# Branch units of a hybrid encoder block: weight sums on VectorE, three blocks of the first branch kept in SBUF, the second branch's blocks stored from GpSimd

## The chip, the core and the metric

The kernel runs on one core of one Trainium2 chip. The metric is the device time of one execution in microseconds. A run of a kernel gives such a time; where several were made their median is quoted. The profile is of one execution, and its times count from the start of that execution's span.

## What is computed

One encoder layer on x of shape (1, 1024, 1024), float32. A single input projection gives u and v of a chunked gating branch, value a and gate g of a convolution branch, and two output gates ga and gb. Each branch ends in a multiplication with a 1024x1024 matrix:

```python
n = rms_norm(h, norm1_g[l])
z = n @ w_in[l]
z_u, z_v, z_a, z_g, z_ga, z_gb = jnp.split(z, split_at, axis=-1)
y_a = spatial_gating(jax.nn.gelu(z_u), jax.nn.gelu(z_v), sg_ln_g[l], sg_ln_b[l],
                     sg_w[l], sg_b[l]) @ w_a_out[l]
y_b = conformer_conv(z_a, z_g, cv_dw_w[l], cv_dw_b[l], cv_ln_g[l], cv_ln_b[l]) @ w_b_out[l]
merged = jax.nn.sigmoid(z_ga) * y_a + jax.nn.sigmoid(z_gb) * y_b
h = h + merged @ w_o[l]
...
h = h + (a feed-forward part with a depthwise convolution of width 3), then a last rms_norm
```

`conformer_conv` is a gated product, a depthwise convolution of width 31, a layer norm over the channels and a silu.

## The kernel before

**Number format.** Every matmul operand is kept as two parts, hi and lo, in a rounded 32-bit type: ScalarE casts the value to hi (L130), VectorE subtracts hi from the value to get lo. A product of two operands is three matmuls, hi x hi, hi x lo and lo x hi. All TensorE and VectorE instructions are recorded through one helper, so their line in the profile is L69; groups are told apart by their tiles. `a`, `w` and `s` are tiles of three pools (`abig`: 16 of 8 KB per partition, `wp`: 3 of 8 KB, `sm`: 15 of 4 KB), `bank` is PSUM. A tile `s` of 128x1024 is 512 KB.

**Projections.** A loop over `order` projects a, g, v, gates, u0 to u7 and then the last six gates, gb2 to gb7. Each projection is 48 matmuls of 128x512. A gate leaves PSUM by a sigmoid on ScalarE (L882) and goes to DRAM (L883); u goes through `evac_u`, and after each odd one `sums_out` is called.

**Branch products.** y_a and y_b are made in eight units, four of `w_a_out` on the first branch (s) and four of `w_b_out` on the second (c, the convolution). A unit covers two column tiles of the weight and is one level of Strassen-Winograd: seven products of 12 matmuls (`strassen`), 84 matmuls in all, instead of eight. Product seven of a unit is put off to stand behind the first product of the next unit. The activation operands are seven blocks, four of them sums of quarters. `sums_out` (L490) makes the sums for two of the eight row tiles with four VectorE instructions of 128x512, and stores all seven blocks to DRAM (`fb_d`) with one transfer of 256 KB and three of 512 KB (L499, L501). It is called four times for each branch: for s with GpSimd's queue, for c with SyncE's. `Blocks` loads them back (L519, two loads of 512 KB per block) and splits them to hi and lo. The block order is 0, 1, 5, 2, 3, 4, 6.

The seven weight operands of a unit are built by `Unit.load` in four steps (L555, L558, L561, L564): SyncE loads quarters of the weight, three times 512 KB and once 256 KB, and after each a GpSimd transfer of 256 KB adds another quarter or an earlier sum to one half of the tile (L566). The same class serves the units of w_o and of the feed-forward part later on.

**The convolution's layer norm** runs in the background of the projections (`conv_norm`, pieces in `bg` and `soon`): a mean by matmul, eight deviations (`dev`), the variance by matmul (`var`), the broadcast of its inverse root by matmul with `ident` (`var2`), eight normalisations `fin` with a multiplication on VectorE and a silu on ScalarE (L743), and after each pair `c_sums` with `sums_out`. A piece is put in where a running model of VectorE's clock has room (`fill`), and the matmuls of `soon` ride in a projection after its third or seventh group. So work added to VectorE earlier moves these pieces later. `conv_d` is the DRAM copy of the deviations, loaded again for `fin` (L697).

**The entry into the units.** In the last three projections `prepare(0..2)` loads s blocks and the first weights and splits them. The stores of c blocks stand in a queue `stores`, emptied after a projection and, one for each, in the `slot` that `strassen` calls after a product. In the products L610 and L617 copy a bank's half, L622 and L627 leave a negated copy in `s`; the next product into that bank waits for them.

## Time and profile before

| | before |
|---|---|
| time, median of 3 runs | 1521.07 us (1520.88 to 1525.44) |
| the profiled execution's own time | 1521.1 us |
| its span in the profile | 1519.0 us |
| TensorE busy | 1464.2 us, 96% of the span, 6633 matmuls |
| VectorE busy | 1007.9 us, 66% |
| ScalarE busy | 629.1 us, 41% |
| GpSimd busy | 165.3 us, 11% |
| SyncE's queue (q1) | 224.63 MB, 42.7% of 16 engines' span |
| GpSimd's queue (q0) | 61.88 MB, 21.8% |

TensorE is busy nearly all the time; the share is an average over stages. The page's row of slices shows full slices up to the entry of the units at about 560 us, and there lower digits for TensorE and for the granted clock, with DMA at nine tenths. The time of a group of transfers is the mean over 16 DMA engines.

### The profile page before, as it was taken

To read this page: it belongs to the slowest core of one execution; us is meant where nothing else is said; L and a number is where in the kernel's file an instruction comes from. 1 tells how busy PE (TensorE), PEld (TensorE's weight loads), DVE (VectorE), ACT (ScalarE), POOL (GpSimd) and SP (SyncE) were. 2 spreads that over 40 slices of the span, in tenths; PEclk is the share of its full clock that TensorE was granted. 3 is DMA by queue.
4 is the path that set the end of the run, shared out by engine and by line. 5 is a ranking of instruction groups with operands and counts; after the bars stand their busy time and mean duration, and the time that the engine had idled before them with its cause. 6 is when DMAs were issued, how large, how long until landed. Compare 5 with 4: busy or idle time off the path is not lost.

```text
span 1519.0 us, 17358 instructions
## 1 busy us (share of the span) xinstructions
PE 1464.2 (96%) x6633; PEld 1213.4 (80%) x6633; DVE 1007.9 (66%) x1047; ACT 629.1 (41%) x763; POOL 165.3 (11%) x200
## 2 busy tenths in 40 slices
PE   9999999999999975999999999999999999999998
PEld 7888888888888864877788888888888887878887
DVE  6899989888998563464553885555555448465545
ACT  6433233443412463353322454444444447353353
POOL 0000000000010001212100011111111211112000
PEclk9999999999999997999999999999999999999999
DMA  5343566445546889999835279777777779999743
GB/s 199 98 109 97 157 178 166 125 125 152 154 128 231 308 282 364 247 357 310 249 100 184 77 182 243 199 202 201 199 202 197 196 190 294 283 361 300 250 173 111
DMA packets 122243, 310.69 MB, mean 205 GB/s; under 512 B 11568, under 2 KB 13872, under 8 KB 122160
## 3 DMA queue, kind: packets, MB, share of 16 engines
q1 hardware_dynamic: 86112, 224.63, 42.7%
q0 software_dynamic: 27392, 61.88, 21.8%
q10 hardware_dynamic: 8656, 23.08, 3.9%
q8 instruction: 52, 0.85, 0.2%
q14 instruction: 31, 0.25, 0.1%
HBM read 199.43 MB, written 76.55 MB: 182 GB/s over the span
## 4 chain that ended last, share of the span: by engine, by line
PE 79%; DMA 7%; DVE 7%; issue 4%; ACT 3%; SPq 1%; POOL 0%; ACTq 0%; DVEq 0%; POOLq 0%
PE bank L69 79%; DVE s L69 5%; DMA s<-fb_d 2%; DMA s<-in_w_a 1%; DMA s<-in_w_b 1%; DMA fb_d<-s 1%; DVE a L69 1%; ACT a L130 1%; DMA s<-h_d 1%; DVE w L69 0%; DMA s<-in_xT 0%; DMA s<-conv_d 0%; ACT w L130 0%; ACT s L743 0%; DMA s<-in_w_down 0%
## 5 line engine op out<-in xcount | busy, mean ns | idle before, releaser
L69 PE MATMUL bank<-a,w 128*128 128x512 f32 (+1 forms) x4158 | 961.7, 391 | 43.5 <-ACT s L622 10.5
L69 PEld LDWEIGHTS bank<-a,w 128*128 128x128 f32 x4158 | 779.2, 190 | 212.2 <-ACT s L622 12.7
L69 PE MATMUL bank<-a,a 128*128 128x512 f32 (+2 forms) x1922 | 413.2, 372 | 2.7 <-ACT s L627 2.0
L69 PEld LDWEIGHTS bank<-a,a 128*128 128x128 f32 x1922 | 340.2, 188 | 68.0 <-ACT s L627 3.3
L69 DVE TENSOR_TENSOR w<-s,w 128x1024 fp32r<-128x1024 f32 (+3 forms) x144 | 162.8, 1132 | 249.7 <-ACT w L130 244.8
L69 DVE TENSOR_TENSOR a<-s,a 128x1024 fp32r<-128x1024 f32 (+2 forms) x180 | 197.7, 1123 | 144.6 <-ACT a L130 144.4
L69 DVE SCALAR_TENSOR_TENSOR s<-hb,vt,s 128x1024 f32<-128x1024 f32 x204 | 247.9, 1277 | 0.0
L130 ACT CAST w<-s 128x1024 fp32r<-128x1024 f32 (+2 forms) x143 | 139.4, 977 | 169.7 <-PE bank L69 87.8
L130 ACT CAST a<-s 128x1024 fp32r<-128x1024 f32 (+2 forms) x148 | 144.3, 995 | 74.5 <-DVE s L69 20.6
L69 DVE TENSOR_TENSOR s<-s,bank 128x1024 f32<-128x1024 f32 (+2 forms) x128 | 110.6, 882 | 36.5 <-PE bank L69 26.3
L566 POOL DMA_DIRECT2D s<-s x72 | 63.5, 881 | 363.5 <-DMA s<-in_w_up 96.0
L69 DVE TENSOR_TENSOR s<-s,s 128x1024 f32<-128x1024 f32 (+1 forms) x74 | 79.0, 1076 | 13.9 <-DMA s<-conv_d 5.1
L69 PE MATMUL bank<-w,a 128*128 128x512 f32 x384 | 87.2, 389 | 0.0
L69 PEld LDWEIGHTS bank<-w,a 128*128 128x128 f32 x384 | 72.1, 188 | 15.0
L566 POOL DMA_DIRECT2D s<-in_w_up x40 | 40.9, 1022 | 260.6 <-DMA s<-in_w_up 232.8
L446 POOL DMA_DIRECT2D s<-s x28 | 24.2, 865 | 370.6 <-ACT s L445 308.8
L69 DVE TENSOR_TENSOR csum<-csum,s 128x1024 f32<-128x1024 f32 (+2 forms) x55 | 45.7, 832 | 22.7 <-ACT s L1387 11.2
L627 ACT ACTIVATE s<-bank 128x512 f32<-128x512 f32 x36 | 21.5, 597 | 79.1 <-PE bank L69 79.1
L610 ACT COPY bank<-bank 128x512 f32<-128x512 f32 x36 | 20.6, 572 | 62.0 <-PE bank L69 61.6
L622 ACT ACTIVATE s<-bank 128x512 f32<-128x512 f32 x36 | 21.4, 594 | 58.2 <-PE bank L69 57.8
L882 ACT ACTIVATE s<-bank 128x1024 f32<-128x1024 f32 x16 | 16.4, 1025 | 69.7 <-PE bank L69 62.0
L1175 ACT ACTIVATE s<-s 128x1024 f32<-128x1024 f32 x22 | 23.3, 1061 | 38.8 <-DVE s L69 38.8
(85 smaller groups left out, 559.6 us busy)
## 6 DMA issues: line engine op xcount, KB each, us to landing
s<-in_w_up SPq DMA_DIRECT2D x64, 512.0 KB, 6.9
s<-fb_d SPq DMA_DIRECT2D x56, 512.0 KB, 9.3
s<-in_w_in SPq DMA_DIRECT2D x39, 512.0 KB, 4.4
fb_d<-s SPq DMA_DIRECT2D x36, 512.0 KB, 3.1
s<-s POOLq DMA_DIRECT2D x72, 256.0 KB, 5.7
s<-s POOLq DMA_DIRECT2D x28, 512.0 KB, 6.5
s<-in_w_down SPq DMA_DIRECT2D x24, 512.0 KB, 8.3
s<-h_d SPq DMA_DIRECT2D x24, 512.0 KB, 8.1
```

The lines of the kernel that those rows point to most:

```text
L69: return fn(*args, **kwargs)
L130: A.copy(dst_hi, src)
L446: G.dma_start(box[k % 2], p, accum_op=ALU.add)
L566: G.dma_start(r[:, 0 if i == 3 else 1], add, accum_op=ALU.add)
L610: A.copy(x[:, 1], x[:, 0])
L622: A.activation(u[:, 0], x[:, 1], AF.Copy, scale=-1.0)
L627: A.activation(u[:, 1], x[:, 1], AF.Copy, scale=-1.0)
L882: A.activation(t, ps.rearrange("p a b -> p (a b)"), AF.Sigmoid)
L1175: A.activation(t, t, AF.Gelu_apprx_tanh)
```

## The change

The change has four parts. **(1)** The eight branch units become `SumUnit`: two plain loads of 512 KB from SyncE per unit (four quarters), and the four sums by VectorE, 128x512 each, two after the split of the first pair of quarters and two after the third split. **(2)** For the s branch, `sums_out` gets `direct`: blocks 0, 1 and 5 in the numbering of the store, the first three of `ORDER`, are split where they are made (three ScalarE copies and three VectorE subtractions of 128x512 per call, four calls), into tiles that stay in SBUF; only the other four blocks are stored, with three transfers per call instead of four, and loaded. **(3)** `c_sums` stores from GpSimd's queue, and what is left in `stores` is issued before the loads behind the last projection. **(4)** `prepare` loads the fourth block and the first unit's two weight tiles, and splits them.

```diff
--- before.py
+++ after.py
@@ -487,13 +487,28 @@
     fb_d = dp.tile([2 + CHUNKS, 7, P, 4, HALF], F32, name="fb_d")
-    def sums_out(t0, t1, c, i, give):
+    def sums_out(t0, t1, c, i, give, direct=None):
         lo, hi = slice(0, HALF), slice(HALF, S)
         sa, sb = sm([P, 2, HALF]), sm([P, 2, HALF])
         V.tensor_tensor(sa[:, 0], t1[:, hi], t0[:, hi], op=ALU.subtract)
         less(sa[:, 1], sa[:, 0], t0[:, lo])
         less(sb[:, 0], sa[:, 1], t1[:, lo])
         V.tensor_tensor(sb[:, 1], t0[:, lo], t0[:, hi], op=ALU.subtract)
+        if direct:
+            parts = [(direct.part(q, i), src) for q, src in enumerate((t0[:, lo], sa[:, 0], t1[:, lo]))]
+            for n, src in parts:
+                A.copy(n[:, 0], src)
+            after_act()
+            for n, src in parts:
+                V.tensor_tensor(n[:, 1], src, n[:, 0].bitcast(F32), op=ALU.subtract)
+            def rest(q):
+                q.dma_start(fb_d[c, 2, :, i], sa[:, 1])
+                q.dma_start(fb_d[c, 3:5, :, i].rearrange("b p c -> p b c"), sb)
+                q.dma_start(fb_d[c, 6, :, i], t1[:, hi])
+            return give(rest)
         def store(q=SP):
             q.dma_start(fb_d[c, 0, :, i], t0[:, lo])
@@ -510,6 +525,11 @@
             self.c = c
             self.raw = {}
             self.n = [[] for _ in range(7)]
+        def part(self, b, i):
+            if i % 2 == 0:
+                self.n[b].append(abig([P, 2, 2, HALF]))
+            return self.n[b][i // 2][:, i % 2]
         def load(self, i):
             if i < 7:
@@ -573,6 +593,35 @@
             split(w[:, 0], w[:, 1], self.raw[i])
             for q in range(n):
                 self.hl[2 * i + q] = w[:, :, q]
+    class SumUnit(Unit):
+        def load(self, i):
+            if i < 2:
+                r = self.raw[i] = sm([P, 2, HALF])
+                SP.dma_start(r, self.src[i].rearrange("p (a k) c -> p a (k c)", a=2))
+        def sums(self, i):
+            (b11, b21), (b12, b22) = [(r[:, 0], r[:, 1]) for r in self.raw[0:2]]
+            t = self.raw[2 + i] = sm([P, 2, HALF])
+            if i == 0:
+                V.tensor_tensor(t[:, 0], b11, b12, op=ALU.add)
+                V.tensor_tensor(t[:, 1], t[:, 0], b22, op=ALU.add)
+            else:
+                V.tensor_tensor(t[:, 0], b12, b22, op=ALU.add)
+                V.tensor_tensor(t[:, 1], self.raw[2][:, 1], b21, op=ALU.add)
+        def split(self, i):
+            n = 1 if i == 2 else 2
+            w = abig([P, 2, n, HALF]) if wn[0] % 5 > 2 else wp.tile([P, 2, n, HALF], F32R, tag="w8", name=nm("w"))
+            wn[0] += 1
+            src, of = [(self.raw[0], (0, 2)), (self.raw[2], (1, 3)), (self.raw[1][:, 1:2], (4,)), (self.raw[3], (5, 6))][i]
+            split(w[:, 0], w[:, 1], src)
+            for q, p in enumerate(of):
+                self.hl[p] = w[:, :, q]
+            if i in (0, 2):
+                self.sums(i // 2)
     wn = [0]
@@ -752,7 +801,7 @@
         def c_sums(j):
             def give(store):
                 def run():
-                    store()
+                    store(G)
                     c_done.append(j)
                 stores.append(run)
@@ -883,6 +932,7 @@
         A.dma_start(gate_d[kind][j], t)
     sT = [None] * KT
+    s_blocks, c_blocks = Blocks(0), Blocks(1)
     def evac_u(ps, j):
         t = sm()
@@ -895,32 +945,25 @@
         V.tensor_tensor(t, t, mix_m[j], op=ALU.mult)
         sT[j] = t
         if j % 2:
-            sums_out(sT[j - 1], t, 0, j // 2, lambda store: store(G))
+            sums_out(sT[j - 1], t, 0, j // 2, lambda store: store(G), s_blocks)
         if j == KT - 1:
             for i in range(KT):
                 mix_m[i] = sT[i] = None
             pair.clear()
-    ab_units = [Unit(w[j : j + 2]) for w in (w_a, w_b) for j in range(0, KT, 2)]
-    s_blocks, c_blocks = Blocks(0), Blocks(1)
+    ab_units = [SumUnit(w[j : j + 2]) for w in (w_a, w_b) for j in range(0, KT, 2)]
     def prepare(n):
         if n == 0:
-            s_blocks.load(0)
-            s_blocks.load(1)
+            s_blocks.load(3)
+            ab_units[0].load(0)
         elif n == 1:
-            ab_units[0].load(0)
-            s_blocks.ahead(0)
-            s_blocks.ahead(1)
+            s_blocks.split(3)
             ab_units[0].load(1)
         else:
             ab_units[0].split(0)
-            s_blocks.split(2)
             ab_units[0].split(1)
-            s_blocks.split(3)
-            ab_units[0].load(2)
-            ab_units[0].load(3)
     for k in range(KT + 1):
         if k < KT:
@@ -975,6 +1018,8 @@
         i += 1
         after_pe()
+    while stores:
+        stores.popleft()()
     s_blocks.load(4)
     s_blocks.load(5)
     ab_units[1].load(0)
```

On TensorE, the place of the broadcast of the convolution's variance (`ident,r`; `ones,csum` is the sum that it rests on). `w_3401` is the third gate projection from the end before, `w_3476` the last but one of the changed kernel. Before:

```order
L69 MATMUL bank_72<-ones,csum 128x1 x8
L69 MATMUL bank_75<-a_463,w_3331 128x512 x6
L69 MATMUL bank_73<-a_432,w_3401 128x512 x6
L69 MATMUL bank_73<-a_435,w_3401 128x512 x6
L69 MATMUL bank_73<-a_439,w_3401 128x512 x6
L69 MATMUL bank_74<-ident,r_3510 128x128 x8
L69 MATMUL bank_73<-a_443,w_3401 128x512 x6
L69 MATMUL bank_73<-a_447,w_3401 128x512 x6
L69 MATMUL bank_73<-a_455,w_3401 128x512 x6
L69 MATMUL bank_73<-a_459,w_3401 128x512 x6
```

After:

```order
L69 MATMUL bank_73<-ones,csum 128x1 x8
L69 MATMUL bank_72<-a_463,w_3392 128x512 x6
L69 MATMUL bank_74<-a_432,w_3476 128x512 x6
L69 MATMUL bank_74<-a_435,w_3476 128x512 x6
L69 MATMUL bank_74<-a_439,w_3476 128x512 x6
L69 MATMUL bank_75<-ident,r_3590 128x128 x8
L69 MATMUL bank_74<-a_443,w_3476 128x512 x6
L69 MATMUL bank_74<-a_447,w_3476 128x512 x6
L69 MATMUL bank_74<-a_455,w_3476 128x512 x6
L69 MATMUL bank_74<-a_459,w_3476 128x512 x6
```

The broadcast stands after the third group of a projection in both, but one projection later, and so do the matmuls of the variance.

On SyncE, the loads and stores at the entry of the first unit: `conv_d` are the deviations, `in_w_a` the weights, `fb_d` the blocks, `ga_d` a gate. Before:

```order
L697 DMA s_3692<-conv_d 128x1024
L697 DMA s_3696<-conv_d 128x1024
L555 DMA s_3714<-in_w_a 128x2x512
L519 DMA s_3723<-fb_d 128x1024
L519 DMA s_3725<-fb_d 128x1024
L519 DMA s_3733<-fb_d 128x1024
L519 DMA s_3735<-fb_d 128x1024
L558 DMA s_3737<-in_w_a 128x2x512
L499 DMA fb_d<-s_3611 128x512
L501 DMA fb_d<-s_3615 128x2x512
L501 DMA fb_d<-s_3700 128x2x512
L501 DMA fb_d<-s_3701 128x2x512
```

After:

```order
L603 DMA s_3718<-in_w_a 128x1024
L746 DMA s_3779<-conv_d 128x1024
L539 DMA s_3817<-fb_d 128x1024
L539 DMA s_3819<-fb_d 128x1024
L539 DMA s_3821<-fb_d 128x1024
L539 DMA s_3823<-fb_d 128x1024
L603 DMA s_3825<-in_w_a 128x1024
L603 DMA s_3827<-in_w_a 128x1024
L1035 DMA s_3830<-ga_d 128x1024
L1035 DMA s_3832<-ga_d 128x1024
L539 DMA s_3861<-fb_d 128x1024
L539 DMA s_3863<-fb_d 128x1024
```

The stores are gone from SyncE, and the weights stand with all loads of blocks behind the convolution's last load.

On GpSimd at the same place; the first rows in each are the last stores of the s branch. Before:

```order
L501 DMA fb_d<-s_3321 128x2x512
L501 DMA fb_d<-s_3322 128x2x512
L566 DMA s_3714<-in_w_a 128x512
L566 DMA s_3737<-s_3714 128x512
L566 DMA s_3817<-in_w_a 128x512
L566 DMA s_3820<-s_3737 128x512
L566 DMA s_3834<-in_w_a 128x512
L566 DMA s_3837<-s_3834 128x512
```

After:

```order
L508 DMA fb_d<-s_3303 128x2x512
L509 DMA fb_d<-s_3298 128x512
L514 DMA fb_d<-s_3674 128x512
L516 DMA fb_d<-s_3676 128x2x512
L516 DMA fb_d<-s_3688 128x2x512
L516 DMA fb_d<-s_3689 128x2x512
L514 DMA fb_d<-s_3680 128x512
L516 DMA fb_d<-s_3684 128x2x512
L516 DMA fb_d<-s_3702 128x2x512
L516 DMA fb_d<-s_3703 128x2x512
```

The accumulations of the weights are gone, and sixteen stores of c blocks stand in their place, of which the first eight are shown.

## Rows read from the trace of the kernel before

**Rows 1.** Stretches: busy (x) PE, PEld, DVE, ACT, POOL; clock, DMA share, GB/s.
```profile
560.00:600.00 40.00, 21.28 (x61) 15.77 (x61) 17.24 (x16) 15.88 (x18) 3.43 (x4) 0.70 0.97 328
600.00:640.00 40.00, 33.32 (x138) 26.84 (x137) 17.80 (x16) 14.67 (x19) 8.74 (x10) 0.91 0.95 271
...
413.00:478.00 65.00, 65.00 (x289) 53.81 (x288) 60.17 (x57) 11.79 (x12) 8.20 (x12) 1.00 0.44 143
...
654.00:703.00 49.00, 43.75 (x185) 35.14 (x184) 33.34 (x30) 26.17 (x32) 6.50 (x8) 0.97 1.02 339
```

**Rows 2.** TensorE's timeline, unit 0: start, duration, what, [idle before <- ended by].
```profile
567.77 5.55 PE L69 MATMUL bank<-a,w 128*128 128x512 f32 x12 [7.91 <-ACT w L130]
...
573.39 2.89 PE L69 MATMUL bank<-a,w 128*128 128x512 f32 x12
581.99 7.82 PE L69 MATMUL bank<-a,w 128*128 128x512 f32 x24 [5.72 <-ACT bank L610]
595.00 5.37 PE L69 MATMUL bank<-a,w 128*128 128x512 f32 x12 [5.19 <-ACT bank L617]
606.60 4.74 PE L69 MATMUL bank<-a,w 128*128 128x512 f32 x12 [6.23 <-ACT s L622]
```

**Rows 3.** Timeline, 529 to 569: the convolution's broadcast, normalisation and sums.
```profile
529.32 1.95 PE L69 MATMUL bank<-ident,r 128*128 128x128 f32 x16
...
532.35 3.50 DVE L69 TENSOR_TENSOR s<-s,s 128x1024 f32<-128x1024 f32 x3 [3.08 <-ACT s L731]
...
538.10 0.68 DVE L69 TENSOR_TENSOR s<-s 128x512 f32<-128x512 f32 x1
...
550.26 1.83 DVE L69 TENSOR_TENSOR s<-s,s 128x1024 f32<-128x1024 f32 x2 [5.14 <-DMA s<-conv_d]
...
558.65 0.68 DVE L69 TENSOR_TENSOR s<-s 128x512 f32<-128x512 f32 x1
...
567.75 1.23 DVE L69 TENSOR_TENSOR w<-s,w 128x1024 fp32r<-128x1024 f32 x1 [3.87 <-ACT w L130]
```

**Rows 4.** Timeline, ScalarE before the sixth product of unit 0.
```profile
603.12 2.94 ACT L130 CAST a<-s 128x1024 fp32r<-128x1024 f32 x3 [5.72 <-DMA s<-in_w_a]
```

**Rows 5.** DMA, 545 to 603: all; queues; issues (count, KB each, us to landing).
```profile
DMA packets 7228, 18.00 MB, mean 310 GB/s; under 512 B 617, under 2 KB 617, under 8 KB 7226
...
q1 hardware_dynamic: 6074, 15.09, 73.3%
q0 software_dynamic: 720, 1.31, 13.0%
...
s<-fb_d SPq DMA_DIRECT2D x10, 512.0 KB, 10.1
...
fb_d<-s SPq DMA_DIRECT2D x6, 512.0 KB, 10.7
...
s<-conv_d SPq DMA_DIRECT2D x1, 512.0 KB, 6.8
```

**Rows 6.** DMA, 413 to 478, among the u projections: GpSimd's queue and its stores.
```profile
q0 software_dynamic: 1536, 5.51, 23.5%
...
fb_d<-s POOLq DMA_DIRECT2D x9, 512.0 KB, 4.2
```

**Rows 7.** Tile fb_d, 400 to 620: issue in ns (min/median/max), us to landing.
```profile
L501 POOL DMA_DIRECT2D fb_d<-s x12: 707/712/731, 427.3 to 501.5; - x12
...
DMA to landing us min/median/max: 2.7/5.2/13.9
```

**Rows 8.** TensorE's timeline, the stops in unit 3.
```profile
675.56 12.60 PE L69 MATMUL bank<-a,w 128*128 128x512 f32 x48 [3.64 <-ACT s L627]
...
691.61 3.01 PE L69 MATMUL bank<-a,a 128*128 128x512 f32 x12 [0.73 <-ACT s L622]
...
698.22 3.02 PE L69 MATMUL bank<-a,a 128*128 128x512 f32 x12 [0.88 <-ACT s L627]
```

**Rows 9.** Groups by form, VectorE's additions of 128x512: busy us, mean ns.
```profile
L69 DVE TENSOR_TENSOR s<-s,s 128x512 f32<-128x512 f32 x20 | 13.5, 687 | 1.8 <-ACT s L743 1.7
```

## The prediction

> **What bounds the kernel now.** I read the table of stretches first [rows 1]. By the page TensorE is busy for 96% of the span, so a change can only give back what TensorE idles, and the idle time is to be found in one place: of 40 us it works 21.28 in 560 to 600 and 33.32 in 600 to 640, with the mean granted clock down to 0.70 and 0.91, while the DMA engines are busy for 0.97 and 0.95 of the time.
>
> Then TensorE's timeline over unit 0, the first of the eight branch units [rows 2]. It starts late (7.91 us, waiting for the hi half of the first weights) and stops before the third, fifth and sixth products (5.72, 5.19 and 6.23 us; the seventh is put off into the next unit). After a stop a product is slow: its 12 matmuls take 5.55, 5.37 or 4.74 us, and 2.89 in the row with no stop ahead. The sixth ends at 606.60 + 4.74 = 611.3.
>
> Third, what came late. The start waits for VectorE's convolution chain: the broadcast matmuls at 529.32, the first normalisation at 532.35, the last sum ending at 558.65 + 0.68 = 559.33, then casts and a gate, and the weights' lo half at 567.75 [rows 3]. The later stops wait for transfers: ScalarE waited 5.72 us for unit 0's weights until 603.12, and its three casts and one evacuation bring the sixth product to 606.60, 3.5 us later [rows 4, 2]. In 545 to 603 the DMA engines moved 18.00 MB and were nearly full [rows 5]. So unit 0 is bound by what has to be moved before it, and by the order in which it is asked for.
>
> **Part 1, weight sums on VectorE.** Per branch unit four accumulating transfers of 256 KB go, and the loads shrink from 1.75 to 1 MB. In 545 to 603 the GpSimd queue, which held the accumulations, took 13.0% of 58 us for 1.31 MB, 5.8 us/MB; SyncE's queue took 73.3% for 15.09 MB, 2.8 us/MB [rows 5]. A unit so frees 5.8 + 0.75 x 2.8 = 7.9 us of DMA time. It adds four sums of 0.69 us, 2.8 us, to VectorE [rows 9]. In 600 to 640, some two units, VectorE works 17.80 of 40 us [rows 1], 9 per unit of 19 us; with 11.8 it still has cover. I count zero outside units 0 and 3; if the cover were gone a unit would lose up to 2.8 us.
>
> **Part 2, three operands kept.** Twelve ScalarE copies and twelve VectorE subtractions of 128x512 enter the u projections. ScalarE is busy for 11.79 of 65 us there, VectorE for 60.17, TensorE for all 65 [rows 1]. The subtractions are 12 x 0.69 = 8.3 us [rows 9]. Over the eight u projections, some 87 us, VectorE comes to 80.5 + 8.3 = 88.8 us, so 0 to 2 us could show. I take 0, since what yields is the convolution's background work, which TensorE needs only later.
>
> It yields at a price: in the changed order the broadcast of the statistics stands one projection later, inside the next to last gate projection in place of the one before it. That is 48 matmuls; 12 take 2.89 us with the first loading shown, about 2.7 in a run, so 10.9 us. The first normalisation moves from 532.35 to 543.2, and 27.0 us of chain follow (532.35 to 559.33) [rows 3]. Two lo halves for the one block that is still loaded early come between, within the 5.14 us that VectorE waited there for a convolution load. Unchanged otherwise, the last sum would end at 570.1. But the four casts, lo halves and the gate that stood between the last sum and the weights no longer do: the weights' lo half follows at once, 1.23 us [rows 3].
>
> **Part 3, stores on GpSimd's queue.** SyncE loses sixteen stores, which stood ahead of weights and blocks. Its loads now wait for landings instead, and all of SyncE stands behind each wait: the last convolution load waits until the first set's third store has landed, the second load for the fifth product until a store of the third set has, the last block's load until the very last store has. The nearest rows for such a store are those of the first branch on the same queue: 0.71 us to issue [rows 7]; in 413 to 478 4.2 us to landing, and 23.5% of 65 us for 5.51 MB, that is 2.8 us/MB [rows 6]; over 400 to 620, both queues, 2.7 to 13.9 us to landing [rows 7]. The convolution blocks' own stores, on SyncE's queue in the crowded stretch, took 10.7 [rows 5]. I take 4.2 for the first set, issued when the crowd hasn't begun, and 6.9 for the last, between the two and nearer the first, since less is moved.
>
> The last convolution load, then: the first set's sums end at 538.8 + 10.9 = 549.7 [rows 3], its third store is out some 2 us later, 551.7, and landed at 555.9; the load lands 6.8 later [rows 5], 562.7, and the chain wants it at 550.26 + 10.9 = 561.1. That is 1.6 us more: the last sum ends at 571.7 and TensorE starts at **573.0**, 5.2 later than now. (Bounds: 3.6, if the load is in time, and 13, if the store takes 13.9.)
>
> What is late next: the first product at the slow clock, 5.55 us, and four of 2.8 bring TensorE to the sixth at 589.8, if the operands are there. Four of the seven blocks are in SBUF by then; the fifth, sixth and seventh products wait for loads, and the evacuation ahead of the sixth stands on ScalarE behind the seventh block's casts. That chain: last sum 571.7; four issues of 0.71, 574.5; landing 6.9, 581.4; the load's landing, 10.1 as for the blocks now [rows 5], 591.5; two casts and the evacuation, 3.5 less one cast of 1, 594.0; the product after a stop, 4.74 [rows 2]: **598.7**. The other bound is volume: from 545 on 14.0 MB must move (stores 7, blocks 3, weights 1.5, convolution 0.5, gates 2) where 18.0 did. At 2.8 us/MB that is 39.2, 584.2, and 2.5 and 4.7 more give 591.4. The chain is later, and I take it: against 611.3, **-12.6 us**. At best TensorE never stops after its start at 571.4, and the sixth ends at 588.2 + 2.9 = 591.1 (-20.2). With 10.7 to landing the sixth ends at 602.5 (-8.8).
>
> One rule speaks against the third part. The rows show plain stores on GpSimd's queue as cheap per MB as SyncE's transfers. The Trainium skill ("DMA: Bandwidth & Descriptors", "Issuing engine by pattern" and "Issuing engines are not separate DMA queues") gives simple loads and stores to SyncE, and says that all issuers' transfers run on the same 16 engines, so that another issuer saves only the issuing. By it the third part is worth at most sixteen issues, and the rest of the gain would have to come from the volume; the sum by volume alone is the -20 above.
>
> **Unit 3**, whose block splits run while it multiplies, loses 3.64 + 0.73 + 0.88 = 5.25 us [rows 8]; the DMA share is 1.02 in 654 to 703 [rows 1]. With 0.75 MB less and no accumulations the blocks are earlier. But VectorE has about 24.8 us of work in that unit (14 lo halves of blocks at 1.2, the weights', the evacuations), and 2.8 more make 27.6 against 19 us of TensorE: at worst 8.6 show, 3.35 more than now. I take -2.5, bounds -5.25 and +3.35.
>
> **Sum**, against the profiled execution's 1521.1 us (span 1519.0; the median is 1521.07, so nothing is to be added): 1521.1 - 12.6 - 2.5 = 1506.0, **1506**.
>
> **The rivals.**
> *VectorE becomes the bound in unit 3*, the engine that takes the sums. For: 27.6 us of work against 19. Against: it works only 33.34 of 49 us in 654 to 703 [rows 1]. It gives 1521.1 - 12.6 + 3.35 = 1511.9.
> *The entry clears wholly*: no stop after the start in unit 0, none in unit 3. For: the volume. Against: the chain of landings. 1521.1 - 20.2 - 5.25 = 1495.7.
> *The stops only change their name.* The last store and the last load take 13.9 us each [rows 7]: 574.5 + 27.8 + 2.5 + 4.7 = 609.5, -1.8, nothing gained in unit 3: 1519.3, no change that can be told. For: the DMA engines were full. Against: 4 MB less.
> *Slower: landings in series on GpSimd's queue.* First set's store out at 551.7, landed 565.6, convolution load 572.4, which is 11.3 us after the chain wants it; last sum 581.4, stores out 584.2, landed 598.1, last block 612.0, sixth product 614.5 where it began at 606.6 before: +7.9, 1529. All at 13.9 us; it decides from about 11.3 a landing, where the sixth begins as before. Against: 4.2 measured on that queue.
> *VectorE starves GpSimd's queue.* Issues on GpSimd lengthen while VectorE works, and the sixteen stores queue up. In the rows they don't: 0.71 us, at most 0.73, with VectorE busy for 60.17 of 65 us [rows 7, 1]. At four times 0.71 the sixteen, begun at 549.7, would be out at 595.1; 6.9, 10.1 and 2.5 more, and the sixth begins at 614.6: +8, 1529. The Trainium skill ("SBUF — State Buffer", "A bandwidth-pool intuition that's wrong") tells of such a lock: 620 ns alone, 3100 ns beside a VectorE copy. No row here shows it.
>
> **How the numbers follow.** Forecast 0.60 (its own range 1498 to 1513), VectorE the bound in unit 3 0.13, entry cleared 0.10, stops renamed 0.08, landings in series 0.06, starved queue 0.03. About 0.3%, 4.6 us, is what a measurement of this kernel can tell from no change. Faster by more: 0.60 + 0.13 + 0.10 = 0.83; within: 0.08; slower: 0.06 + 0.03 = 0.09. The range goes from 1495 (the entry cleared) to 1516 (-8.8 at the entry, +3.35 in unit 3), and leaves out the last three cases, 0.17.
>
> **What would show it.** The first product of unit 0 should start at 571 to 576 and the sixth end at 591 to 603, with stops only before the fifth and sixth, both traced to ScalarE behind a block load. GpSimd's sixteen issues should stay at 0.6 to 0.7 us, with landings under 11. The DMA share in 560 to 640 should fall below 0.95. In unit 3 the stops should be at most 5 us, ended by a cast that waited for a block, not by VectorE. The prediction is wrong if TensorE waits in the u projections, if the first product starts after 577, or if another unit gets a stop of over 1 us that ends with VectorE.

## The result and the profile after

The changed kernel took 1504.33 us (median of 4, 1502.72 to 1505.0) against 1523.26 for the kernel before beside it: ratio 0.9872, 95% interval 0.9847 to 0.9898, some 19 us less. Run once more in other company (`after_again`, below) it gave 0.9883, 0.9864 to 0.9902. The profiled execution has a span of 1500.9 us where the one before had 1519.0.

The table of stretches of the changed kernel, in the columns of [rows 1]:

```profile
560.00:600.00 40.00, 26.36 (x90) 20.18 (x89) 27.71 (x32) 22.04 (x25) 4.14 (x6) 0.74 0.89 337
600.00:640.00 40.00, 40.00 (x178) 33.13 (x177) 20.85 (x23) 13.24 (x18) 0.00 (x0) 1.00 0.54 193
```

TensorE works 5 us more in the first 40 us and all of the second; the DMA share there has fallen from 0.97 and 0.95 to 0.89 and 0.54. Where unit 0 now stops is seen in TensorE's timeline of the changed kernel, to be held against [rows 2]:

```profile
540.63 1.95 PE L69 MATMUL bank<-ident,r 128*128 128x128 f32 x16
...
568.24 1.22 PE L69 MATMUL bank<-a,w 128*128 128x512 f32 x2 [7.70 <-ACT w L130]
571.22 15.85 PE L69 MATMUL bank<-a,w 128*128 128x512 f32 x58 [1.76 <-DVE w L69]
591.25 5.49 PE L69 MATMUL bank<-a,a 128*128 128x512 f32 x12 [4.18 <-ACT s L671]
...
651.93 16.71 PE L69 MATMUL bank<-a,w 128*128 128x512 f32 x72 [0.41 <-ACT s L671]
...
673.48 3.04 PE L69 MATMUL bank<-a,a 128*128 128x512 f32 x12 [2.04 <-ACT s L671]
...
733.58 4.49 PE L69 MATMUL bank<-a,w 128*128 128x512 f32 x12 [2.66 <-ACT s L671]
738.75 31.57 PE L69 MATMUL bank<-a,w 128*128 128x512 f32 x137 [0.69 <-ACT s L676]
```

The last two places in the kernel before, in unit 7 and behind it:

```profile
752.17 3.04 PE L69 MATMUL bank<-a,w 128*128 128x512 f32 x12 [1.75 <-ACT s L622]
755.89 4.37 PE L69 MATMUL bank<-a,w 128*128 128x512 f32 x18 [0.69 <-ACT s L627]
```

The broadcast is at 540.63 in place of 529.32. Two matmuls need only the weights' hi half and start at 568.24; the others wait for VectorE's lo half until 571.22. From there five products run without a stop. One stop is left, 4.18 us before the sixth, and the sixth ends at 596.74, where it ended at 611.34: -14.6 us. Unit 3's stops are 0.41 and 2.04 us in place of 5.25 [rows 8], and unit 7's stop of 1.75 has become 2.66. The matmuls behind it begin at 738.75, where in the kernel before they began at 755.89, so 17.1 us of the 18.1 in the span lie ahead of that place. I have not traced the last microsecond.

What holds the sixth product is read from the waits of SyncE's queue between 545 and 600, from ScalarE's timeline, and from what one store needed to land. Waits first (us in total, times, longest), changed kernel:

```profile
SPq L539 <- DMA fb_d<-s: 10.9, 2, 6.1
SPq L603 <- DVE s L69: 7.8, 3, 6.7
SPq L539 <- DVE a L69: 7.3, 1, 7.3
```

Loads of blocks (L539) waited 10.9 us in all for stores to land, 6.1 us the longest; loads of weights (L603) waited for VectorE. The tile `fb_d` in 570.3 to 571.5, which is the last store alone (duration of the issue in ns, then us to landing), changed kernel:

```profile
L516 POOL DMA_DIRECT2D fb_d<-s x1: 710/710/710, 570.4 to 570.4; - x1
...
DMA to landing us min/median/max: 13.4/13.4/13.4
```

The timeline behind it, changed kernel:

```profile
580.55 3.64 SPq L539 DMA_DIRECT2D s<-fb_d  x2
...
587.89 1.04 ACT L130 CAST a<-s 128x1024 fp32r<-128x1024 f32 x1 [4.29 <-DMA s<-fb_d]
...
589.66 1.04 ACT L130 CAST a<-s 128x1024 fp32r<-128x1024 f32 x1 [0.72 <-DMA s<-fb_d]
590.61 0.59 ACT L671 ACTIVATE s<-bank 128x512 f32<-128x512 f32 x1
```

The last store is issued at 570.44 and lands at 583.8. The second of the last two block loads takes the buffer that this store reads, goes out then (580.55 + 3.64 is the end of its issue) and lands 5.8 us later, at 589.7. The cast of what it brought follows, the other load's cast having run at 587.89, and then the evacuation L671, as the prediction had it. (The last gate's store, 575.93 and 7.8 us to landing, ends at 583.7, and that load waits for it too: it would have held it as long.) The evacuation of the fourth product stands on ScalarE behind casts for the seventh product, and the sixth waits for it.

### The profile page after: what moved, and what is told of

Read it like the earlier page. It is cut to its first block, busy times and chain, and to the rows that moved or that the text cites. A ratio compares the mean times of both kernels' runs of the same rounds, so it can differ in the third digit from the quotient of the medians.

```text
span 1500.9 us, 17240 instructions
## 1 busy us (share of the span) xinstructions
PE 1460.4 (97%) x6634; PEld 1211.4 (81%) x6634; DVE 1027.2 (68%) x1085; ACT 630.3 (42%) x769; POOL 144.5 (10%) x180
## 4 chain that ended last, share of the span: by engine, by line
PE 79%; DVE 9%; DMA 5%; issue 3%; ACT 3%; SPq 1%; ACTq 0%; DVEq 0%; POOLq 0%
PE bank L69 79%; DVE s L69 7%; DMA s<-fb_d 2%; DVE a L69 2%; DMA s<-in_w_down 1%; DMA fb_d<-s 1%; ACT a L130 1%; DMA h_d<-s 1%; DVE w L69 0%; DMA s<-in_xT 0%; DMA s<-h_d 0%; ACT w L130 0%; ACT s L792 0%; SPq L539 0%; DVE hb L69 0%
## 5 line engine op out<-in xcount | busy, mean ns | idle before, releaser
L69 PE MATMUL bank<-a,a 128*128 128x512 f32 (+2 forms) x1934 | 419.0, 374 | 7.1 <-ACT s L671 6.2
L69 PEld LDWEIGHTS bank<-a,a 128*128 128x128 f32 x1934 | 344.3, 189 | 73.5 <-ACT s L671 7.1
L130 ACT CAST a<-s 128x1024 fp32r<-128x1024 f32 (+2 forms) x142 | 138.7, 996 | 66.8 <-DVE s L69 19.2
L69 DVE TENSOR_TENSOR s<-s,s 128x1024 f32<-128x1024 f32 (+1 forms) x98 | 95.4, 980 | 10.4 <-ACT s L780 7.9
L586 POOL DMA_DIRECT2D s<-s x56 | 49.4, 882 | 269.5 <-DMA s<-in_w_up 87.2
L676 ACT ACTIVATE s<-bank 128x512 f32<-128x512 f32 x36 | 21.5, 598 | 93.9 <-PE bank L69 93.8
L446 POOL DMA_DIRECT2D s<-s x28 | 24.3, 866 | 371.0 <-ACT s L445 309.2
L671 ACT ACTIVATE s<-bank 128x512 f32<-128x512 f32 x36 | 21.5, 597 | 60.3 <-PE bank L69 57.6
```

What stands on the lines that cost most here:

```text
L69: return fn(*args, **kwargs)
L130: A.copy(dst_hi, src)
L446: G.dma_start(box[k % 2], p, accum_op=ALU.add)
L586: G.dma_start(r[:, 0 if i == 3 else 1], add, accum_op=ALU.add)
L671: A.activation(u[:, 0], x[:, 1], AF.Copy, scale=-1.0)
L676: A.activation(u[:, 1], x[:, 1], AF.Copy, scale=-1.0)
```

## The experiments

All ratios are to the kernel before in the same runs, with its median near 1524 us, so 0.001 is 1.5 us.

**The parts, one by one.** `p1_only` is the kernel before with the weight sums on VectorE, and nothing else.

```diff
-    ab_units = [Unit(w[j : j + 2]) for w in (w_a, w_b) for j in range(0, KT, 2)]
+    ab_units = [SumUnit(w[j : j + 2]) for w in (w_a, w_b) for j in range(0, KT, 2)]
```

> The kernel before with the weight sums on VectorE alone; the blocks are all stored and loaded, stores stay on SyncE. My theory (volume and landings bind the entry, the accumulations are the dearest transfers): most of the gain is here. The sixth product of unit 0 ends 8 to 14 us earlier than the 611.3 of before, unit 3 loses about 2.5 in place of 5.25: 1507 to 1513, ratio 0.989 to 0.994. Rival (the gain is in the blocks that stay on chip and the stores that leave SyncE): 1517 to 1521, ratio above 0.997.

Measured: 1513.75 us, ratio 0.9925 (0.9905 to 0.9945). The ratio is within what my theory gave, the time 0.75 us above it. The sixth product starts at 599.76, 6.8 us earlier than the 606.60 of before, where I had said 8 to 14 for its end; unit 3 stops 2.67 us. Sums alone bring some 11 us.

`p3_only` is the kernel before with GpSimd storing the convolution's blocks.

```diff
-                    store()
+                    store(G)
                     c_done.append(j)
```

> The kernel before with the convolution's blocks stored from GpSimd, weights still built by accumulating transfers on the same queue. My theory (what binds is volume and the wait for landings, and the accumulations now queue behind the stores on GpSimd): -4 to +5 us, ratio 0.997 to 1.003. Rival (SyncE's order holds the loads, and moving the stores frees it): 1507 to 1513, ratio 0.989 to 0.994.

Measured: 1524.67 us, ratio 0.9992 (0.9979 to 1.0005): nothing. In TensorE's timeline of this kernel the stop before the third product is shorter (2.38 us), and those before the fifth and sixth are longer than the 5.19 and 6.23 of before:

```profile
597.03 4.49 PE L69 MATMUL bank<-a,w 128*128 128x512 f32 x12 [10.36 <-ACT bank L617]
608.44 5.49 PE L69 MATMUL bank<-a,w 128*128 128x512 f32 x12 [6.92 <-ACT s L622]
```

The accumulation that the fifth product's weights need is issued at 577.45, right behind eight stores on the same queue (570.22 to 575.9), and takes 16.1 us to land; before, it was issued at 584.34 and took 7.2. Loads in the same stretch took 12 to 14 us too, so how much of this is the queue and how much the crowd is not shown. With accumulations and stores on one queue, the move only changed who waits.

`no_p3` is the changed kernel with the one line of `p3_only` taken back.

> The changed kernel with the convolution's blocks stored from SyncE. My theory (SyncE stands behind each set's sums, so block loads that now go out at 561 to 569 go out after the last sum's stores, at 573 or later): the fifth product gets a stop of 1 to 4 us, the sixth product ends 2 to 8 us later than the 596.7 of the changed kernel: ratio 0.989 to 0.993. Rival, after the Trainium skill (DMA: Bandwidth & Descriptors, Issuing engines are not separate DMA queues): another queue saves only the issuing, so the time is within 1.5 us of the changed kernel's, ratio 0.987.

Measured: 1518.02 us, ratio 0.9959 (0.9944 to 0.9974). The rival that the time stays within 1.5 us is out: it is 12 to 14 us above the changed kernel. My theory had the direction, but two thirds of the size at most, and the wrong place. Not the fifth product stops but the first starts late. TensorE's timeline, and SyncE's waits in 536 to 600, of `no_p3`:

```profile
579.98 1.22 PE L69 MATMUL bank<-a,w 128*128 128x512 f32 x2 [18.91 <-ACT w L130]
582.96 16.27 PE L69 MATMUL bank<-a,w 128*128 128x512 f32 x58 [1.76 <-DVE w L69]
604.66 5.24 PE L69 MATMUL bank<-a,a 128*128 128x512 f32 x12 [5.43 <-ACT s L671]
```

```profile
SPq L603 <- DVE a L69: 17.8, 1, 17.8
```

On SyncE the load of unit 0's second weights waits 17.8 us for a buffer that VectorE frees only with the first lo half of the fourth block. In this kernel the stores of the first two sets and the last convolution load stand behind it: the first store goes out at 560.85, in the changed kernel at 546.49. VectorE's chain waits for the convolution load, and so the sums and the first weights do. The two loads in `no_p3`, and then in the changed kernel with the first set's third store:

```profile
560.47 0.33 SPq L603 DMA_DIRECT2D s<-in_w_a  x1
...
569.14 1.29 SPq L746 DMA_DIRECT2D s<-conv_d  x1
```

```profile
549.09 0.73 POOL L516 DMA_DIRECT2D fb_d<-s  x1 [0.55 <-DVE s L69]
...
550.17 0.33 SPq L603 DMA_DIRECT2D s<-in_w_a  x1
...
553.41 0.32 SPq L746 DMA_DIRECT2D s<-conv_d  x1
```

The one line changes more than the queue. In the changed kernel the same load of weights gets another buffer of the pool, that of a convolution tile, and waits only 6.7 us (the line `SPq L603 <- DVE s` above); in `no_p3` that tile's store stands behind this load. Of the 15.7 us by which the last convolution load is later, 10.3 are the longer wait for the buffer. The rest comes from the eight store issues between the two loads, 8.3 us, where the changed kernel waited 2.8 for a store to land. So the 12 to 14 us are not the price of the queue alone, and what would be left with the same buffer no run shows.

The Trainium skill ("DMA: Bandwidth & Descriptors", "Issuing engines are not separate DMA queues") lets another issuer save only the issuing. The sixteen issues on SyncE took 0.36 to 1.59 us each here, some 18 us in all, so the size of the loss does not go against it. The transfers themselves are indeed no cheaper: 2.8 us/MB on GpSimd's queue and 2.7 on SyncE's, in 545 to 590 of the changed kernel. What comes on top is the wait in front of the stores, which SyncE's queue handed to all that stood behind it.

`no_p2` is the changed kernel without the kept operands.

```diff
-            sums_out(sT[j - 1], t, 0, j // 2, lambda store: store(G), s_blocks)
+            sums_out(sT[j - 1], t, 0, j // 2, lambda store: store(G))
...
         if n == 0:
-            s_blocks.load(3)
-            ab_units[0].load(0)
+            s_blocks.load(0)
+            s_blocks.load(1)
         elif n == 1:
-            s_blocks.split(3)
+            ab_units[0].load(0)
+            s_blocks.ahead(0)
+            s_blocks.ahead(1)
             ab_units[0].load(1)
         else:
             ab_units[0].split(0)
+            s_blocks.split(2)
             ab_units[0].split(1)
+            s_blocks.split(3)
```

> The changed kernel without the operands kept on chip: the first branch stores and loads all seven blocks, prepare as in the kernel before. My theory of the late start (work added to VectorE in the u projections pushes the convolution's broadcast one projection later): the broadcast is back at 529 and unit 0 starts at 566 to 569 in place of 571.2. What that gains is lost again to 1.5 MB more loads behind 545, so the sixth product ends at 593 to 600 and the time is within 4 us of the changed kernel's: ratio 0.985 to 0.990. Rival (the kept blocks carry the gain): the entry is as in p1_only or later, 5 us or more above the changed kernel, ratio above 0.990.

Measured: 1501.34 us, ratio 0.9847 (0.9829 to 0.9865). So the kept operands bring nothing on top of the other two parts; by their ratios the two runs of the changed kernel, 0.9872 and 0.9883, lie 4 to 5.5 us above, with intervals that overlap for the one and just touch for the other. TensorE's timeline of `no_p2`:

```profile
530.49 1.95 PE L69 MATMUL bank<-ident,r 128*128 128x128 f32 x16
...
562.75 0.73 PE L69 MATMUL bank<-a,w 128*128 128x512 f32 x2 [1.72 <-ACT w L130]
...
576.32 1.22 PE L69 MATMUL bank<-a,w 128*128 128x512 f32 x2 [9.50 <-ACT w L130]
578.65 12.95 PE L69 MATMUL bank<-a,w 128*128 128x512 f32 x46 [1.11 <-DVE w L69]
592.50 8.50 PE L69 MATMUL bank<-a,a 128*128 128x512 f32 x36 [0.89 <-ACT s L671]
```

The broadcast is back at 530, as it should be if the added work in the u projections had moved it. Unit 0's first two matmuls start 5.5 us earlier than in the changed kernel (562.75 against 568.24), and earlier than I gave; its second product then stops for 9.50 us; the sixth begins at 592.50, against 591.25. Two quite different entries meet at the same place, the landing of the last block.

In all: sums alone 0.9925, stores alone 0.9992, both 0.9847. The stores are worth some 12 us once the accumulations are gone, and nothing before. (`no_p2` and the changed kernel also empty `stores` ahead of the loads behind the last projection, which is the other half of part 3. `p1_only` and `p3_only` lack it, `no_p3` keeps it, and no run tests it alone.) Where these 12 us come from is seen in the stores of the tile `fb_d` in 536 to 600 (count, issue in ns, first and last start), `p1_only` and then `no_p2`:

```profile
L501 SPq DMA_DIRECT2D fb_d<-s x12: 359/360/1578, 537.6 to 572.4; - x12
```

```profile
L516 POOL DMA_DIRECT2D fb_d<-s x12: 707/708/728, 537.6 to 557.2; - x12
```

On GpSimd the last store goes out 0.4 us after the last sum ends (556.74). On SyncE it goes out 10.3 us after it (562.10), since the last two sets stand behind four block loads whose issues, with their waits, took from 553.63 to 564.71. An issue on SyncE's queue is the shorter one here, 0.36 us in the median against 0.71.

**Is it the chain to the sixth product?** `late_split` is the changed kernel with the seventh product's casts put behind the evacuation.

```diff
         def ahead(self, i):
-            if i < 3:
-                s_blocks.ahead(4 + i)
+            if i in (0, 1, 3):
+                s_blocks.ahead((4, 5, 0, 6)[i])
```

> The changed kernel, with the last block's casts put after the sixth product's evacuation on ScalarE, not ahead of it. My theory (the 4.18 us stop before the sixth product, and its slow clock after it, come from that evacuation standing behind casts which wait for the last block's load, and that load waits for the last store's landing): the stop goes, the sixth product begins at 586 to 588 and takes 2.9 us, unit 1 begins 4 to 7 us earlier than 596.7, with at most 2 us of stop before the seventh product: ratio 0.982 to 0.985, that is 4 to 6 us under the changed kernel. Rival (the sixth product's own operands are late, or the landing of the last store holds the seventh product just as long): within 2 us of the changed kernel, ratio 0.986 to 0.988.

Measured: 1498.54 us, ratio 0.9829 (0.9811 to 0.9848). TensorE's timeline of `late_split`:

```profile
571.60 15.76 PE L69 MATMUL bank<-a,w 128*128 128x512 f32 x58 [1.76 <-DVE w L69]
587.20 2.89 PE L69 MATMUL bank<-a,a 128*128 128x512 f32 x12
589.92 0.40 PE L69 MATMUL bank<-a,ones_r 128*128 128x512 f32 x1
```

The stop is gone, and the product runs in 2.89 us and not in 5.49; unit 1 begins 6.6 us earlier. The seventh product, now the one that follows the late block's casts, does not stop either. The sixth product's own operands had been there. The wait was an order on ScalarE.

`warm` fills the gap ahead of unit 0 with matmuls that nobody reads. (It did the same before unit 1, where I had not meant it to.)

```diff
                 PE.matmul(ps[:, h], ones_r, a11(0, 0), start=True, stop=True, skip_group_check=True)
+                for _ in range(48 if h else 0):
+                    nc.tensor.matmul(ps[:, h], ones_r, a11(0, 0), start=True, stop=True, skip_group_check=True)
```

> The changed kernel with 48 extra matmuls in the gap before unit 0, into a bank that is overwritten before it is read; they need only an operand that is kept on chip. They fill 560 to 571 and so keep the granted clock up. My theory (the sixth product's start is set by a chain of landings, not by TensorE): the first products are 2.5 us faster, the stop before the sixth grows by as much, and the time is within 1.5 us of the changed kernel: ratio 0.986 to 0.989. Rival (TensorE's slow clock after the gap is on the path): 2 to 3 us less, ratio 0.985 to 0.986.

Measured: 1515.21 us, ratio 0.994 (0.992 to 0.996). TensorE's timeline of `warm`:

```profile
562.55 11.30 PE L657 MATMUL bank<-a,ones_r 128*128 128x512 f32 x48
573.69 14.09 PE L69 MATMUL bank<-a,w 128*128 128x512 f32 x60
593.00 4.35 PE L69 MATMUL bank<-a,a 128*128 128x512 f32 x12 [5.22 <-ACT s L673]
...
597.42 11.32 PE L657 MATMUL bank<-a,ones_r 128*128 128x512 f32 x48
```

The ratio misses my forecast, since the second block of 48 costs its full 11.3 us; without it the time would be 1503.9, that of the changed kernel. That is worked out, not measured, and its interval is too wide to rule out the rival's 2 to 3 us. The trace says more. The granted clock was 0.96 of full speed in 560 to 600 in place of 0.74, and sixty matmuls took 14.09 us where fifty-eight had taken 15.85. The sixth product still starts 50.2 us after the broadcast (542.80), where the changed kernel took 50.6 us, and 51.5 in its second run (`after_again`, where the broadcast is at 539.99):

```profile
591.46 5.11 PE L69 MATMUL bank<-a,a 128*128 128x512 f32 x12 [5.11 <-ACT s L671]
...
673.93 4.61 PE L69 MATMUL bank<-a,a 128*128 128x512 f32 x12 [2.03 <-ACT s L671]
```

The stop by itself proves little: it grew from 4.18 to 5.22 us with the matmuls, but it was 5.11 in `after_again` without them. A faster engine ahead of this wait reaches it sooner and waits.

`late_warm_once` puts the same 48 matmuls into `late_split`, before unit 0 only.

```diff
-                for _ in range(48 if h else 0):
+                for _ in range(extra.pop() if extra else 0):
...
+    extra = [48]
```

> late_split with the 48 extra matmuls in the gap before unit 0 only. In the run warm they stood before unit 1 too, which cost their 11.3 us; without these its time was that of the changed kernel, though its first products were 2 us shorter. My theory: that gain was lost in the stop before the sixth product, and as this stop is gone in late_split, the same matmuls now gain 1 to 3 us on it: ratio 0.981 to 0.9825. Rival (the block loads behind the seventh product set the end all the same): ratio 0.9825 to 0.984, as late_split.

Measured: 1496.02 us, ratio 0.9817 (0.9798 to 0.9835), in my theory's range but not to be told from `late_split`. In the trace the gain of unit 0 is given back by a stop of 1.34 us in unit 1 (at 594.24, ended by L679). I leave it open.

**The entry without the kept operands.** `no_p2_early` takes `no_p2` and asks for unit 0's second weights ahead of four block loads.

```diff
             ab_units[0].load(0)
+            ab_units[0].load(1)
             s_blocks.ahead(0)
             s_blocks.ahead(1)
-            ab_units[0].load(1)
```

> The kernel without the operands kept on chip, with unit 0's second weight load asked for ahead of four block loads and not behind them. In that kernel the second product stops for 9.5 us, since its weights' load was issued only after a store had landed. My theory (the last block's landing sets the end of the entry, about 592 for the sixth product's start): the second product's stop goes, but the third to sixth wait in its place, and the time stays within 2 us of 1501: ratio 0.983 to 0.986. Rival (that stop is on the path by itself): 5 to 8 us less, ratio under 0.981.

Measured: 1499.57 us, ratio 0.9834 (0.9813 to 0.9856). The stop before the second product falls from 9.50 to 3.94 us, and the one before the sixth rises from 0.89 to 3.35. The rival, 5 to 8 us, is out.

`no_p2_early_late` adds the edit of `late_split`.

> The same with the last block's casts put after the sixth product's evacuation as well. If my theory of the two is right, both stops go together where neither edit alone gains all: the sixth product begins by 588, unit 1 by 592, ratio 0.979 to 0.983. Rival (the entry is bound by the amount of data alone): no less than without it, ratio 0.983 to 0.986.

Measured: 1495.35 us, ratio 0.9813 (0.9787 to 0.9839). The stop before the sixth is gone, as in `late_split`. Its median is the lowest of the study; it beats both kernels, by some 29 and 10 us. From `late_split` and `late_warm_once` it can't be told.

`after_again` is the changed kernel, unedited.

> The changed kernel once more, in more rounds and beside the next three, to have its distance to them and to no_p2 on one scale. Forecast: ratio 0.986 to 0.989. If my theory is right that the operands kept on chip cost more than they bring once the stores are on GpSimd's queue, the interval lies above no_p2's 0.9847; the rival is that the two are one.

Measured: 1506.07 us, ratio 0.9883 (0.9864 to 0.9902). Its interval lies above `no_p2`'s 0.9847, as expected, but overlaps that run's interval (0.9829 to 0.9865) by 0.0001. Taken alone, the first run of the changed kernel can't be told from `no_p2`. That the kept operands cost something is likely, by some 0 to 5 us, and no more than that.

**Units 3 and 7.** The 2.04 us stop in unit 3 of the changed kernel ends with ScalarE; what ScalarE did before it, changed kernel:

```profile
670.37 1.41 DVE L69 TENSOR_TENSOR s<-s,s 128x512 f32<-128x512 f32 x2
...
671.89 1.04 ACT L130 CAST w<-s 128x1024 fp32r<-128x1024 f32 x1 [3.53 <-DVE s L69]
...
672.84 0.59 ACT L671 ACTIVATE s<-bank 128x512 f32<-128x512 f32 x1
```

The cast ahead of the evacuation waits 3.53 us for VectorE's weight sums, which the change has added. `evac_first` puts that evacuation ahead of all casts at its place, in every unit of the kernel.

```diff
-        slot(2)
         product(x[:, 1], w.hl[3], s2, False)
         A.activation(u[:, 0], x[:, 1], AF.Copy, scale=-1.0)
+        slot(2)
         slot(3)
```

> The changed kernel with the evacuation after the fourth product put ahead of all casts of that place, in every unit. In unit 3 the sixth product stops 2.04 us and in unit 7 2.66 us for that evacuation; before it on ScalarE stands a cast that waits 3.5 us for VectorE's weight sums (unit 3), or casts that wait for VectorE's last gates. My theory: these stops are order on ScalarE, as in unit 0; they go, with the slow clock behind some of them: 4 to 9 us under late_split, ratio 0.977 to 0.981. Rival (VectorE itself is the bound there, and the next product waits in place of this one): within 2 us of late_split, 0.982 to 0.984.

Measured: 1497.95 us, ratio 0.9839 (0.9816 to 0.9862): the theory's 4 to 9 us under `late_split` did not come, and the rival's number did. The trace shows both at work. TensorE's timeline of `evac_first`:

```profile
652.58 11.19 PE L69 MATMUL bank<-a,w 128*128 128x512 f32 x48 [2.32 <-ACT s L676]
...
725.32 3.01 PE L69 MATMUL bank<-a,w 128*128 128x512 f32 x12 [1.71 <-ACT s L670]
729.02 41.33 PE L69 MATMUL bank<-a,w 128*128 128x512 f32 x180 [0.69 <-ACT s L676]
```

Up to 729.02 it is 5.6 us ahead of `late_split`, which reaches that place at 734.59. Then it loses most of them: in a feed-forward unit near 1250, two stops of 1.96 us (L671) and 1.30 us (L676) in `late_split` become one of 4.01 us for L676, and the 24 matmuls after it take 8.58 us where they took 5.75. The lead is 4.3 us ahead of that place and 1.0 behind it, and the spans end 1.6 us apart. The casts that were taken from in front of one evacuation now stand in front of the next. `best` is the same edit on `no_p2_early`.

> The same edit on the kernel without operands kept on chip and with unit 0's weights asked for earlier (no_p2_early). If the edits gain apart from each other: 4 to 8 us under no_p2_early_late, 1488 to 1492, ratio 0.974 to 0.979. If VectorE is the bound in units 3 and 7: as no_p2_early_late, 0.980 to 0.983.

Measured: 1497.57 us, ratio 0.9827 (0.9807 to 0.9848): no gain, like `evac_first`.

## Why the prediction was right, point by point

Forecast 1506, measured 1504.3; the spans differ by 18.1 us, where the sum had 15.1. The terms:

- **The start of unit 0.** Predicted 573.0, seen 571.22, with two matmuls ahead at 568.24, which is below the 571 to 576 of the text's own sign. The shift of one projection is as counted, and `no_p2` bears out its cause. TensorE did not wait in the u projections, as assumed: it is busy for all of 400 to 560. The first set's third store went out at 549.09 and not at 551.7, since GpSimd issues each store as its sum is done and not after the set; the convolution load, which waits for its landing, was out at 553.41, 4.3 us later, which is the 4.2 taken from the u projections [rows 6].
- **The chain to the sixth product.** Predicted start 594.0, seen 591.25, end 598.7 against 596.74, so -14.6 where -12.6 was said. The chain is the predicted one, but that its end came out within 2 us is partly luck, since its terms were mis-sized and nearly cancel. The last store took 13.4 us to land and not 6.9: that is near the upper end of [rows 7], the price in two of the rivals, and above the 11 that the text allowed. The load behind it took 5.8 and not 10.1. The last sum ended 1.7 us earlier than said, and its last store was issued 0.4 us behind it and not after four issues, 2.8 us. The fifth product, which I had stopping too, did not stop.
- **A row misread.** The text has ScalarE wait 5.72 us for unit 0's weights [rows 4]. In the kernel before unit 0's weights are four tiles, `s_3714`, `s_3737`, `s_3817` and `s_3820`, and the tile of that cast is the next, `s_3834`, which is unit 1's first. So in the kernel before, too, the sixth product's evacuation stood on ScalarE behind a cast made ahead for a later product, and the wait was one for an accumulation, which part 1 removes.
- **Volume against chain.** I took the chain as the later bound, and the experiments bear it out. `late_split` moves as much, 16.42 MB in 545 to 592 against 16.54, and its sixth product begins 4.0 us earlier. `no_p2_early` moves more, 17.50 MB in 545 to 590 against 15.71, and begins 2.6 us earlier. (The DMA engines were nonetheless full in 560 to 591, at a share of 1.03, and the long landing of the last store falls there.)
- **Unit 3.** Predicted -2.5, seen 5.25 - 2.45 = -2.8. But the reason was half wrong. I wrote that a cast waiting for a block would end the stop, not VectorE; it is a cast that waits for VectorE's sums. The rival on VectorE named the engine rightly and priced it too high.
- **The units counted at zero.** Unit 7's stop is 2.66 us in every kernel that has the sums on VectorE without `evac_first`'s order (in `p1_only`, `no_p2`, `no_p3` too), and 1.75 in `p3_only` as before: 0.9 us, and at times a slow product behind it. Ahead of the evacuation stands a cast that waits 3.68 us for VectorE; in the kernel before it waited 3.74, so why the stop is longer is not shown. The text's own sign of an error, another unit with a stop over 1 us that hangs on VectorE, is met there, though the stop is not new; the cost is small.
- **Stores on GpSimd.** Sixteen issues at 0.54 to 0.73 us, with VectorE busy for 36.92 of 47 us in 545 to 592; the starved queue did not come. In 545 to 590 GpSimd's queue took 45.3% of 45 us for 7.34 MB, 2.8 us/MB as priced. The changed kernel's DMA in 545 to 590, in the columns of [rows 5]:

```profile
q0 software_dynamic: 2048, 7.34, 45.3%
q1 hardware_dynamic: 2005, 7.30, 43.7%
...
fb_d<-s POOLq DMA_DIRECT2D x12, 512.0 KB, 7.8
...
s<-fb_d SPq DMA_DIRECT2D x6, 512.0 KB, 7.7
```

- **What the sum did not see.** It treated the three parts as one gain. They are not additive: sums -11 us, stores 0 alone and -12 with the sums, kept operands 0 to +5. And the stores' worth has no term of its own in the sum; the text bounds it by sixteen issues, by the rule, or by volume. In `p1_only` and `no_p3` it was above all waiting on SyncE's queue: stores behind loads that waited for a buffer, and what stood behind the stores.

## What to carry to other kernels

Follow an operand back through every queue it stands in: the engine's that casts it, the queue's that loads it, and the store that frees its buffer; a wait at the head of an in-order queue is paid by all behind it, and stores that stand behind such a wait can be worth moving to another queue. Such a move can also change which buffer a load gets, so look at that load's wait in both kernels before the gain is put down to the queue. Taking a cause away helps only if it is the last one at its place, so try edits in pairs as well as alone: the stores gained nothing until the accumulations were gone, and warmed matmuls gained nothing ahead of a stop. Before work is added to an engine that is busy for 93% of a stretch, look at what is in the background there, since that is what will be late.

## What the runs showed of the hardware that I had not expected

- A 512 KB store from GpSimd's queue took 13.4 us to land where the median of its kind in the same stretch was 7.8; the end of such a chain hangs on the slowest and not on the median.
- After a stop of about 2.0 us at the same place in unit 3, the next 12 matmuls took 3.04 us in one execution of the changed kernel, at a granted clock of 1.00 of 2.4 GHz, and 4.61 in the other, at 0.62 in the mean. After the stop of 0.69 us none was slow. What a stop costs so varies by some 1.5 us from one execution to the next, which no edit here made.
- With matmuls in the gap the granted clock in 560 to 600 was 0.96 in place of 0.74; it followed what TensorE had done just before, whatever the matmuls were for. Without them, TensorE worked 1.56 of 11 us up to 571.2, and the clock was 0.50, the lower level of 1.2 GHz, in 571.2 to 576.0 and 0.98 in 576 to 587.
